# Two gates' clamp on GpSimd, a later start of layer 0's first attention head, and another order of the last sums, in a two-layer hybrid decoder

## The chip, the cores and the metric

The kernel runs on one core of a Trainium2 chip. The metric is the device time of one execution in microseconds (us), the median over the runs; smaller is better. Engines are named as in the profile: PE is the matrix engine (TensorE) and PEld its weight loads, DVE is VectorE, ACT is ScalarE, POOL is GpSimd, SP is SyncE, which issues most DMAs.

## What is computed

Two layers over 528 tokens (16 learned meta tokens and 512 real ones) with 1024 features, all in float32. The reference, cut to what matters:

```python
def hybrid_layer(h, attn_norm_g, w_in, b_fgate, ret_gn_g, w_out, ...):
    xn = rmsnorm(h, attn_norm_g)
    proj = jnp.einsum('bld,dc->blc', xn, w_in)
    fq, fk, fv, flog, rq, rk, rv, rg = jnp.split(proj, SPLIT_POINTS, axis=-1)
    logf = jax.nn.log_sigmoid(flog + b_fgate)
    fox_out = fox_attention(fq, fk, fv, logf)        # 8 heads of 64: softmax with a decay
    rq_ = rotate(rq, cos, sin)
    rk_ = rotate(rk, cos, sin) * (RET_HEAD_DIM ** -0.5)
    ret = retention_chunkwise(rq_, rk_, rv)          # 4 heads of 128: no softmax
    ret = head_groupnorm(ret, ret_gn_g)
    ret_out = jax.nn.silu(rg) * ret
    h = h + jnp.einsum('blc,cd->bld', jnp.concatenate([fox_out, ret_out], -1), w_out)
    hn = rmsnorm(h, ffn_norm_g)
    ff = jax.nn.silu(hn @ w_gate) * (hn @ w_up)
    return h + ff @ w_down

def reference(x, meta_tokens, ...):
    ...
    for i in range(DEPTH):
        h = hybrid_layer(h, ...)
    return rmsnorm(h, final_norm)[:, N_META:]
```

## The kernel before

Features lie on the 128 partitions and tokens along the free dimension. Each float32 operand is split into a high part, rounded to the fp32r type, and a low part, and a product takes three matmuls: high by high, high by low, low by high. A dense projection (L225) is a row of eight *chunks*, one per 128 input features. In layer 0 a chunk is six matmuls, three products for each of two halves of 264 tokens; in layer 1, where only the 512 real tokens go on, a chunk of some projections is three matmuls of 512 columns.

**Weights.** A DMA on SP brings a weight block to `raw`; ACT rounds it to `whi` in two halves (L199), and for most projections of the attention stage POOL subtracts `wlo = raw - whi` in eight pieces of 128 columns (L202). This is called ahead for the next projection, so that PE finds the parts ready.

**Attention.** A pair of softmax heads ("fox") is cut into steps: `scores` for the queries of one head and one block (PE L524 into a PSUM tile of the ring `psa`, which has four buffers; DVE L528 subtracts the mask and finds the row's minimum `nmax`; ACT L541 takes exponentials), `values` (PE transposes L427 of `pd`; ACT L505 and DVE L506 split them into `vv`), `turn` (PE transposes of the exponentials `pr`; ACT L150 and DVE L151 split them into `pth`, `ptl`), and `product` (PE L594, then ACT L597 and DVE L598). The keys `kc` of a head carry the forget gates' sums, put there by DVE L472 or ACT L469 for the first pair and by POOL L467 for the later ones.

**Retention.** A head's steps are `values` (transposes L427; DVE L690 takes means and L691 subtracts them), `scores` (PE L727; DVE L732 multiplies by the decay into `sd`; ACT L150 and DVE L151 split it into `rsh`, `rsl`), `product` (PE L761), then `weigh`, `head_norm` and `gate`. The gate projection of a head ends in `g_done` (L653): DVE L655 scales it into `sg`. For heads 2 and 3 ACT then applies silu. For heads 0 and 1, which run beside softmax exponentials, silu is built from exponentials: DVE L664 writes `ge = max(sg, -80)`, ACT L665 takes `exp(-ge)`, L666 a logarithm and L667 an exponential. The clamp keeps the exponential finite. Heads 0 and 1 run in each of the two layers, so L664 runs four times.

**Order.** PE runs exactly the order of the written plan. A list of dense chunks is the base, and `merge` puts the other steps in front of the chunk with the number that stands as their place; `spread(main, a, b)` spaces the first part of a fox pair's steps evenly from place a to b, and `ret_places` gives each step of a retention head its place. For the other engines a scheduler orders instructions by its own estimates, except those that are pinned; each engine then runs its own order strictly, waiting at an instruction for its semaphores.

**The end.** The last norm takes its statistics in two parts of 272 and 240 tokens. For the second, ACT squares each of the eight blocks `h[m]` (`square_b`, L1140). DVE adds some of the squares into an accumulator (`sum_b`, L1143); the accumulator and the remaining squares are added over partitions by plain float32 matmuls with a matrix of ones (L1169), each of which is two passes on PE. ACT takes the root (L1157), DVE refines it in three instructions (L1161, L1163, L1165) and multiplies the output (L1147), and SP stores it.

Of the kernel before, what the change touches and what calls it, by code (L numbers as in the profile page):

```python
# [13 lines left out]
ALU = mybir.AluOpType  # L14

D = 1024
NK = D // 128
# [22 lines left out]
def hybrid_kernel(ctx, tc, x_t, w_in, w_fl, w_out, w_gate, w_up, w_down, vecs, b_fg, rope, decay, mask, ident, out_t):  # L40
    nc = tc.nc
# [75 lines left out]
    def repeat(vt, c0, n, at):  # L117
        nc.scalar.copy(vt[:, at:at + 32 * n].rearrange("p (n c) -> p n c", c=32)[:, :, 0:META],
                       vt[:, c0:c0 + META].unsqueeze(1).broadcast_to([128, n, META]))
# [10 lines left out]
    def sv(t, real, p0=0, p1=128):  # L130
        if real:
            return t[p0:p1, META:T]
        return t[p0:p1, 0:T].rearrange("p (a b) -> p a b", a=2)

    def pv(ps, real, p0=0, p1=128):
        if real:
            return ps[p0:p1, 0, 0:SEQ]
        return ps[p0:p1, :, 0:HALF]
# [10 lines left out]
    def split(hi, lo, src, pinned=False):  # L149
        pin(nc.scalar.copy(hi, src), pinned)  # L150
        pin(nc.vector.tensor_sub(lo, src, hi.bitcast(F32)), pinned)  # L151
# [53 lines left out]
    def dense_steps(src, parts, pool=False, banks=False, ahead=(1, 4), own=None, wait=None):  # L205

        j = len(jobs)
        jobs.append({"src": src, "pool": pool, "own": own})  # L210

        def chunk(k0, k, n, xs, cols, ps, done):
            def go():
                convert(j)
                if k == 0:
                    t = [psum_a() for _ in cols] if banks else psum()
                    ps.append(t)
                    ps.append(t if banks else [t[:, b] for b in range(2)])
                size = jobs[j]["w"][0][0]
                _, hi, lo = jobs[j]["w"][(k0 + k) // size]  # L220
                wk = (k0 + k) % size
                xh, xl = xs(k)
                for i, (w, x) in enumerate(((hi, xh), (hi, xl), (lo, xh))):
                    for b, (c0, c1) in enumerate(cols):
                        nc.tensor.matmul(ps[1][b][:, 0:c1 - c0], w[:, wk, :], x[:, c0:c1],  # L225
                                         start=(k == 0 and i == 0), stop=(k == n - 1 and i == 2))
                if k == n - 1:
                    done(ps[0]) if wait is None else wait.append((ps[0], done))
                for half, at_step in enumerate(ahead):
                    if k0 + k == at_step:  # L230
                        convert(j + 1, 4 * half + 4)
            return go

        steps = []
        for k0, xs, n, cols, done in parts:
            ps = []
            steps += [chunk(k0, k, n, xs, cols, ps, done) for k in range(n)]
        return steps
# [35 lines left out]
    def tt(name, dt=F32):  # L274
        tag, bufs = tags[name]
        return tmp.tile([128, T], dt, name=name, tag=tag, bufs=bufs)

    def at(tag, dt=F32R, shape=(128, T), bufs=None):
        return phase["att"].tile(list(shape), dt, name=tag, tag=tag, bufs=bufs)

    def fft(tag, dt=F32R, shape=(128, T), bufs=None):
        return phase["ffn"].tile(list(shape), dt, name=tag, tag=tag, bufs=bufs)
# [32 lines left out]
    def pin(f, pinned=True):  # L315
        if pinned:
            tc.keep_in_program_order(f)
# [97 lines left out]
    def silu(t, then=None):  # L415
        nc.scalar.activation(t, t, AF.Silu)
        if then:
            tc.keep_in_program_order(nc.scalar.preload_act_table_set(then))
# [210 lines left out]
    def ret_dense(l, hd, ly, real, st, which):  # L629
        QC = REAL if real else FULL  # L630

        def rope_done(nm, rl):
            def go(ps):
                xsw = tt("xsw")
                nc.scalar.copy(sv(xsw, rl, 0, 64), pv(ps, rl, 64, 128))
                nc.scalar.copy(sv(xsw, rl, 64, 128), pv(ps, rl, 0, 64))
                nc.vector.tensor_mul(sv(xsw, rl), sv(xsw, rl), sv(ly["sr"], rl))
                t1 = tt("tq")
                nc.vector.tensor_mul(sv(t1, rl), pv(ps, rl), sv(ly["cr"], rl))
                nc.vector.tensor_add(sv(t1, rl), sv(t1, rl), sv(xsw, rl))  # L640
                th = at(nm + "h")
                tl = at(nm + "l")
                split(sv(th, rl), sv(tl, rl), sv(t1, rl))
                st[nm] = (th, tl)
            return go

        def v_done(ps):
            vr = v_tiles[1]
            nc.vector.scalar_tensor_tensor(sv(vr, False), pv(ps, False), RSC, sv(ly["R"], False), ALU.mult, ALU.mult)
            repeat(vr, SEQ, 2, SEQ + 32)  # L650
            st["vr"] = vr

        def g_done(ps):  # L653
            sg = tt("sg")
            nc.vector.scalar_tensor_tensor(sv(sg, real), pv(ps, real), RSC, sv(ly["R"], real), ALU.mult, ALU.mult)  # L655
            st["sg"] = sg
            if hd > 1:
                silu(sv(sg, real), LOGS)
                return


            u, v = sv(tt("ge"), real), sv(at("gr", F32), real)
            x = sv(sg, real)
            nc.vector.scalar_tensor_tensor(u, x, -80.0, x, ALU.max, ALU.max)  # L664
            nc.scalar.activation(u, u, AF.Exp, scale=-1.0)  # L665
            nc.scalar.activation(v, u, AF.Ln, bias=onec)  # L666
            nc.scalar.activation(v, v, AF.Exp, scale=-1.0)  # L667
            st["open"] = u, v, x

        base = 3 * FP + 4 * hd  # L670
        job = {"q": (0, QC, rope_done("rq", real)), "k": (1, FULL, rope_done("rk", False)),
               "v": (2, FULL, v_done), "g": (3, QC, g_done)}
        return sum([dense_steps(w_in[l, base + job[c][0]], [(0, lambda k: ly["x"][k], NK, job[c][1], job[c][2])], True)
                    for c in which], [])
# [150 lines left out]
    def ffn(l, st, real, last):  # L825
# [235 lines left out]
        for r, (f0, f1) in enumerate(ROUNDS):  # L1061
            for f in range(f0, f1):
# [4 lines left out]
                u = Unit(f)  # L1067
# [27 lines left out]
        else:  # L1095
# [4 lines left out]
            na, nb = PA[1] - PA[0], PB[1] - PB[0]  # L1100
            fin = {}
# [28 lines left out]
            def square_b(m):  # L1130
                if m == 0:
                    t = fft("S", F32, (128, 6, w), 2)
                    fin["one"] = [t[:, i, 0:nb] for i in range(2)]
                    fin["acc"], fin["rb"], fin["tb"] = (t[:, i, 0:nb] for i in range(3, 6))
                    d = fin["acc"]
                elif m < NK - 2:
                    fin["sq", m] = d = tt("sq")[:, 0:nb]
                else:
                    d = fin["one"][m - NK + 2]
                pin(nc.scalar.activation(d, h[m][:, cb], AF.Square))  # L1140

            def sum_b(m):
                pin(nc.vector.tensor_add(fin["acc"], fin["acc"], fin["sq", m]))  # L1143
# [23 lines left out]
            def sums(v, parts):  # L1167
                for i, t in enumerate(parts):
                    nc.tensor.matmul(v, ones if t.dtype == F32R else ones.bitcast(F32), t, start=(i == 0), stop=(i == len(parts) - 1))  # L1169
# [51 lines left out]

            def after_7():
                square_b(7)
                sum_b(5)
                v = psum_a()[:, 0:nb]
                sums(v, [fin["one"][0], fin["acc"], fin["one"][1]])
                out_a(2)
                out_a(4)
                out_a(6)
                scale_b(3)  # L1230
                root(fin["rb"], v)
                scale_b(4, 5, 6, 7)
                for i in range(3):
                    newton(i, fin["rb"], v, fin["tb"])
                for k in range(0, NK, 2):
                    out_b(k)

            end = NK * n
            places = [(end, after_a)] + [(end + n * (i + 1), f) for i, f in enumerate(
                (after_0, after_1, after_2, after_3, after_4, after_5, after_6, after_7))]  # L1240
# [11 lines left out]
    def layer(l):  # L1252
# [57 lines left out]
        q, k, v = fd(0)  # L1310
# [19 lines left out]
        sums = [lambda: forget_sums(l, ly)]  # L1330
# [11 lines left out]

        for g in range(2):
            main, rest = fs[g]
            m0, r0, places = (((7 if l else 11, 31 if l else 32.5), (34, 40.5), (13, 33.5, 35.5, 37.5, 39, 40.5, 43, 44, 47.5, 48)),
                              ((0.5, 31.5), (32, 40), (13, 33.5, 35.5, 39.5, 39, 41.5, 43, 44, 47.5, 48)))[g]
            plan += merge(rd(g, "vqkg") + sum(fd(g + 1), []),
                          spread(main, *m0), spread(rest, *r0), ret_places(g, *places))
# [92 lines left out]
```

## Time and profile before

| | |
|---|---|
| median of 3 runs | 1268.45 us (1268.43 to 1269.03) |
| the profiled execution's own time | 1268.51 us |
| its span, from the first to the last instruction | 1266.7 us |
| mean granted TensorE clock | 0.998 |
| busy: PE / PEld / DVE / ACT / POOL | 99% / 94% / 79% / 56% / 22% |
| read from HBM, written | 112.58 MB, 2.10 MB |

The span is what the trace covers; 1.8 us of the execution's time lie around it. In a row of the timeline the columns are the start and the duration in us, the engine, the line in the kernel, the operation, what is written and read, the shapes, how many instructions are merged into the row, and in brackets the engine's idle time in front of it and what ended it. A row of the waits names the engine that waited, the line at which it waited and for whom, then the sum, the number and the longest of the waits.

### The profile page before, as it was taken

The page shows a single profiled execution, that of the slowest core. Times are in us where ns is not written, and L with a number is a line of the kernel's source. Part 1 is how long each engine was busy: PE and PEld are TensorE (multiplying, and loading weights), DVE is VectorE, ACT ScalarE, POOL GpSimd, SP SyncE. Part 2 cuts the span into 40 slices and gives each one's busy share as a digit, 9 for nine tenths or more (in the row PEclk, how much of TensorE's full clock was granted, in tenths as well). Part 3 has the DMA queues.
Part 4 walks back from the last instruction along what each step waited for, and adds up shares of the span by engine and source line. Part 5 has one row for each costly group of instructions (what it writes and reads, how often), then busy time and mean ns, then how long its engine had stood idle before and what let it go on. Part 6 is the DMA issues. An engine that isn't in the chain of part 4 may idle for free.

```text
span 1266.7 us, 23528 instructions
## 1 busy us (share of the span) xinstructions
PE 1250.7 (99%) x9223; PEld 1192.2 (94%) x9223; DVE 994.4 (79%) x1800; ACT 706.2 (56%) x1305; POOL 274.3 (22%) x540
## 2 busy tenths in 40 slices
PE   9999999999999999999999999999999999999997
PEld 9999999999999999999999989998789999999996
DVE  8887756879988888887786877567899888888867
ACT  7767655676444444444466665557764444444445
POOL 3555546420000000000126556554100000000000
PEclk9999999999999999999999999999999999999999
DMA  6212222223333333332322122222233333333321
GB/s 218 67 60 69 83 76 73 71 67 117 105 97 100 100 101 100 101 101 84 101 77 84 61 84 74 71 89 67 100 96 121 100 101 101 100 101 101 100 84 67
DMA packets 43342, 116.19 MB, mean 92 GB/s; under 512 B 5088, under 2 KB 12000, under 8 KB 43232
## 3 DMA queue, kind: packets, MB, share of 16 engines
q1 hardware_dynamic: 42800, 114.41, 28.1%
q8 instruction: 72, 1.18, 0.4%
q14 instruction: 38, 0.31, 0.1%
q10 hardware_dynamic: 432, 0.29, 0.1%
HBM read 112.58 MB, written 2.10 MB: 91 GB/s over the span
## 4 chain that ended last, share of the span: by engine, by line
PE 91%; DVE 4%; ACT 4%; issue 1%; DMA 0%; ACTq 0%; DVEq 0%
PE psd L225 28%; PE psa L912 18%; PE psd L1047 14%; PE psd L912 13%; PE psa L225 5%; PE psa L1047 4%; PE psa L427 2%; PE psa L524 1%; PE psa L594 1%; PE psa L761 1%; PE psa L727 1%; ACT whi L199 1%; PE psa L298 0%; ACT xh L327 0%; DMA raw<-w_in 0%
## 5 line engine op out<-in xcount | busy, mean ns | idle before, releaser
L202 POOL TENSOR_TENSOR wlo<-raw,whi 128x128 fp32r<-128x128 f32 x504 | 259.1, 548 | 256.0 <-ACT whi L199 235.3
L225 PE MATMUL psd<-xh,whi 128*128 128x264 f32 (+1 forms) x792 | 195.5, 314 | 0.0
L225 PE MATMUL psd<-xh,wlo 128*128 128x264 f32 (+1 forms) x792 | 186.9, 304 | 0.0
L225 PE MATMUL psd<-xl,whi 128*128 128x264 f32 (+1 forms) x792 | 186.4, 303 | 0.4 <-DVE xl L328 0.4
L225 PEld LDWEIGHTS psd<-xh,whi 128*128 128x128 f32 x792 | 128.5, 190 | 4.9 <-ACT whi L199 0.5
L225 PEld LDWEIGHTS psd<-xh,wlo 128*128 128x128 f32 x792 | 127.0, 188 | 6.3 <-DVE wlo L202 0.4
L225 PEld LDWEIGHTS psd<-xl,whi 128*128 128x128 f32 x792 | 127.6, 189 | 5.1 <-DVE xl L328 1.1
L199 ACT CAST whi<-raw 128x512 fp32r<-128x512 f32 (+1 forms) x168 | 97.9, 613 | 41.7 <-PE psd L225 28.6
L900 ACT CAST whi<-raw 128x1024 fp32r<-128x1024 f32 (+2 forms) x62 | 54.8, 885 | 51.2 <-PE psd L912 39.8
L900 ACT CAST fwhi<-raw 128x1024 fp32r<-128x1024 f32 (+2 forms) x62 | 55.6, 897 | 48.0 <-PE psd L912 40.5
L122 POOL MEMSET kc<- 64x528 f32 x2 | 1.1, 532 | 345.4 <-PE psa L912 345.4
L901 DVE TENSOR_TENSOR wlo<-raw,whi 128x1024 fp32r<-128x1024 f32 (+2 forms) x62 | 62.9, 1015 | 12.6 <-ACT whi L900 12.5
L901 DVE TENSOR_TENSOR fwlo<-raw,fwhi 128x1024 fp32r<-128x1024 f32 (+2 forms) x62 | 64.0, 1033 | 11.0 <-ACT fwhi L900 10.7
L912 PE MATMUL psa<-th,whi 128*128 128x264 f32 (+1 forms) x232 | 65.4, 282 | 0.0
L912 PE MATMUL psa<-th,wlo 128*128 128x264 f32 (+1 forms) x232 | 65.4, 282 | 0.0
L912 PE MATMUL psa<-tl,whi 128*128 128x264 f32 (+1 forms) x232 | 65.3, 282 | 0.0
L912 PE MATMUL psa<-th,fwhi 128*128 128x264 f32 (+1 forms) x224 | 63.4, 283 | 0.0
L912 PE MATMUL psa<-tl,fwhi 128*128 128x264 f32 (+1 forms) x224 | 63.3, 283 | 0.0
L912 PE MATMUL psa<-th,fwlo 128*128 128x264 f32 (+1 forms) x224 | 63.2, 282 | 0.0
L541 ACT ACTIVATE pr<-pr,nmax 128x144 f32<-128x144 f32 (+1 forms) x64 | 36.8, 575 | 44.4 <-DVE nmax L528 25.7
L900 ACT CAST fwhi<-S 128x1024 fp32r<-128x1024 f32 x20 | 21.0, 1049 | 68.6 <-PE psa L912 66.5
L978 ACT COPY e<-psa 128x264 f32<-128x264 f32 (+1 forms) x114 | 42.9, 376 | 28.3 <-PE psa L912 24.1
(368 smaller groups left out, 4044.8 us busy)
## 6 DMA issues: line engine op xcount, KB each, us to landing
raw<-w_in SPq DMA_DIRECT2D x54, 512.0 KB, 3.5
raw<-w_gate SPq DMA_DIRECT2D x44, 512.0 KB, 4.0
fraw<-w_up SPq DMA_DIRECT2D x38, 512.0 KB, 3.5
raw<-w_down SPq DMA_DIRECT2D x64, 256.0 KB, 2.9
raw<-w_out SPq DMA_DIRECT2D x16, 512.0 KB, 3.5
raw<-w_down SPq DMA_DIRECT2D x32, 192.0 KB, 2.5
raw<-w_up SPq DMA_DIRECT2D x6, 512.0 KB, 3.5
h<-x_t SPq DMA_DIRECT2D x8, 264.0 KB, 4.5
```

The costliest lines, as they stand in the source:

```text
L199: pin(nc.scalar.copy(hi, job["raw"][:, c0:c1]), pinned)
L202: pin(sub(lo[:, c:c + step], job["raw"][:, c0 + c:c0 + c + step], hi[:, c:c + step].bitcast(F32)), pinned)
L225: nc.tensor.matmul(ps[1][b][:, 0:c1 - c0], w[:, wk, :], x[:, c0:c1], start=(k == 0 and i == 0), stop=(k == n - 1 and i == 2))
L427: nc.tensor.transpose(ps[:, 128 * j:128 * j + 128], src[:, o:o + 128], idt)
L524: nc.tensor.matmul(sc[0:nq, 0:c1 - c0], qq[:, q0:q0 + nq], kk[:, c0:c1], start=(i == 0), stop=(i == 1))
L541: nc.scalar.activation(pr, pr, AF.Exp, bias=nmax[0:nq], scale=-1.0, accum_out=rsum)
L594: nc.tensor.matmul(po[:, c0:SEQ], v[:, j, :], pp[:, j, META + c0:T], start=(j == 0 and i == 0), stop=(j == 4))
L900: nc.scalar.copy(hi, src)
L901: nc.vector.tensor_sub(lo, src, hi.bitcast(F32))
L912: nc.tensor.matmul(bank()[:, 0:b.shape[-1]], a[:, o + k, :], b, start=(fresh and k == 0 and i == 0), stop=(k == n - 1 and i == 2), skip_gr ...
L978: nc.scalar.copy(self.t["e"][:, i], self.t["x"][:, 0:w])
L1047: nc.tensor.matmul(v[:, 0:c1 - c0], a[:, s * n + k, :], b[:, c0:c1], start=(k == 0 and i == 0), stop=(k == n - 1 and i == 2))
```

## The change

Three edits. The clamp L664 moves from DVE to POOL, and from an instruction that reads `sg` twice to one that reads it once with a constant. In layer 0 the first fox pair's steps start at place 12 instead of 11 and end at 33 instead of 32.5, and the first retention head's `values` moves from place 13 to 16.5; layer 1 keeps its places. At the end three squares (of blocks 5, 6 and 7) instead of two (6 and 7) go to PE as they are, so DVE makes one addition less and PE one float32 matmul more.

```diff
-            nc.vector.scalar_tensor_tensor(u, x, -80.0, x, ALU.max, ALU.max)
+            nc.gpsimd.tensor_scalar_max(u, x, -80.0)
...
-                    fin["one"] = [t[:, i, 0:nb] for i in range(2)]
+                    fin["one"] = [t[:, i, 0:nb] for i in range(3)]
...
-                elif m < NK - 2:
+                elif m < NK - 3:
                     fin["sq", m] = d = tt("sq")[:, 0:nb]
                 else:
-                    d = fin["one"][m - NK + 2]
+                    d = fin["one"][m - NK + 3]
...
                 square_b(7)
-                sum_b(5)
                 v = psum_a()[:, 0:nb]
-                sums(v, [fin["one"][0], fin["acc"], fin["one"][1]])
+                sums(v, [fin["one"][0], fin["acc"]] + fin["one"][1:])
...
-            m0, r0, places = (((7 if l else 11, 31 if l else 32.5), (34, 40.5), (13, 33.5, 35.5, 37.5, 39, 40.5, 43, 44, 47.5, 48)),
+            m0, r0, places = (((7 if l else 12, 31 if l else 33), (34, 40.5), (13 if l else 16.5, 33.5, 35.5, 37.5, 39, 40.5, 43, 44, 47.5, 48)),
```

What this does to the engines' orders, at three places. First PE in layer 0, where the first fox pair begins. `psd` rows are dense chunks (two rows of high weights and one of low weights make one chunk), `kc` rows are the scores of the pair's first head, `pd_115` are the fox values and `pd_116` the retention values.

```order
-L524 MATMUL psa<-kc_105,qo_103 16x16
-L524 MATMUL psa<-kx_462,qs_453 16x16
 L225 MATMUL psd<-xh_185,whi 128x264 x2
 L225 MATMUL psd<-xl_186,whi 128x264 x2
 L225 MATMUL psd<-xh_185,wlo 128x264 x2
+L524 MATMUL psa<-kc_105,qo_103 16x16
+L524 MATMUL psa<-kx_462,qs_453 16x16
 L225 MATMUL psd<-xh_193,whi 128x264 x2
 L225 MATMUL psd<-xl_194,whi 128x264 x2
 L225 MATMUL psd<-xh_193,wlo 128x264 x2
```

The first scores stand one chunk later, and so do the pair's following steps up to its first `product`; the retention values, which stood right behind the 128x144 scores, now stand behind the 128x272 scores and one more chunk. From the scores that follow that product on, PE's order is the same as before up to the end.

Second, POOL in layer 1, at the gate of the first retention head: the eight pieces of one weight block are a run of eight rows of L202.

```order
 L467 TENSOR_SCALAR kc_8392<-fs,pick 40x528
-L202 TENSOR_TENSOR wlo<-raw,whi 128x128 x40
+L202 TENSOR_TENSOR wlo<-raw,whi 128x128 x8
+L664 TENSOR_SCALAR ge<-sg 128x512
+L202 TENSOR_TENSOR wlo<-raw,whi 128x128 x32
```

The clamp stands behind a whole weight block of eight pieces. In layer 0 the first clamp stands in the same way behind the eight pieces that follow `kc_106`; the second head's clamps stand behind one piece in layer 0 and two in layer 1.

Third, ACT at the same place in layer 1; these rows are the changed kernel's, and before, ACT had them in this order too, with the last two the other way round.

```order
L575 CAST pth<-pe 16x4x16
L665 ACTIVATE ge<-ge 128x512
L150 CAST pth<-psa 128x2x128
L666 ACTIVATE gr<-ge,onec 128x512
L150 CAST rsh<-sd 128x512
L667 ACTIVATE gr<-gr 128x512
L150 CAST pth<-psa 128x3x128
L150 CAST rsh<-sd 128x400
```

L665 now waits for POOL instead of DVE, and the cast to `rsh`, which PE's first retention product L761 needs, is queued behind it. At the same place in layer 0 ACT had L665, L541, L666, L551, L667, `rsh`; it now has L541, L665, L551, L666, `rsh`, L667.

## The prediction

> **What bounds the kernel now.** I read the page's first part and the chain of work that ended last, then the stages, then what PE waited for in each stage.
>
> ```profile
> PE 1250.7 (99%) x9223; PEld 1192.2 (94%) x9223; DVE 994.4 (79%) x1800; ACT 706.2 (56%) x1305; POOL 274.3 (22%) x540
> PE 91%; DVE 4%; ACT 4%; issue 1%; DMA 0%; ACTq 0%; DVEq 0%
> 275.35 20.64 PE psd L225 x168
> 30.00:80.00 50.00, 46.04 (x362) 43.95 (x361) 41.51 (x99) 34.82 (x86) 23.02 (x46) 1.00 0.18 59
> 690.00:710.00 20.00, 19.72 (x117) 17.11 (x116) 15.56 (x33) 13.62 (x30) 9.12 (x18) 1.00 0.21 67
> ```
>
> PE is busy 99% of the span and carries 91% of the chain. Its work is fixed by the plan and hardly changes here. So nothing counts but the gaps in PE's row, and the tail behind its last matmul. DVE's and POOL's busy time alone are worth nothing. The chain's third row gives PE's pace: 168 matmuls in 20.64 us, 0.123 us each, so a chunk of six is 0.73 us. The two stages show where the change can act: PE idles 50.00 - 46.04 = 3.96 us between 30 and 80 us (layer 0, first pair), and 0.28 us between 690 and 710 us (the same place in layer 1). These are PE's waits there, in the order stage of layer 0 (eight rows), layer 1 (one), end (one):
>
> ```profile
> PE psa L727 <- DVE ptl L151: 1.0, 1, 1.0
> PE psa L524 <- DVE kc L472: 0.8, 1, 0.8
> PE psa L594 <- DVE ptl L151: 0.7, 1, 0.7
> PE psa L427 <- DVE sd L732: 0.4, 1, 0.4
> PE psa L524 <- DVE sq L691: 0.4, 1, 0.4
> PE psa L761 <- DVE rsl L151: 0.2, 1, 0.2
> PE psa L761 <- ACT rsh L150: 0.2, 1, 0.2
> PE psa L427 <- DVE nmax L528: 0.2, 1, 0.2
> PE psa L761 <- DVE rsl L151: 0.3, 1, 0.3
> PE psa L1169 <- ACT S L1140: 0.9, 1, 0.9
> ```
>
> A stall costs about 0.2 to 0.25 us more than its idle time. A matmul stands in the record with some 0.3 us, although the next one starts 0.12 us behind it.
>
> **Layer 0 up to the product.** The pair's first scores waited for `kc` (0.8 idle, about 0.95 lost). Now a further chunk, 0.73, stands in front of them, while `kc` comes when it did: 0.2 stays, gain 0.75. The next two waits (0.2 for `nmax`, 0.4 for the retention values' L691, together about 1.05 lost) were for PSUM buffers that the retention values had taken between the fox scores. They now come behind two more steps, but new short waits replace them: the fifth retention transpose needs the 128x272 scores reduced, and the 128x400 scores need the fox values' last split. I walked DVE and ACT in their new order with the durations of their rows and get 0.15 and 0.35: gain 0.55. The product's wait for the last `ptl` (0.7 idle, 0.95 lost) has one more chunk in front of it, and its inputs follow from the same scores some 1.3 us earlier, behind a DVE row relieved of the retention values' early place; I take all of it, with 0.5 us to spare. Together 0.75 + 0.55 + 0.95 = **2.25 us** by the time PE reaches the second head's last scores; bounds 0.75 (the two unsure parts give nothing) and 2.7.
>
> **Layer 0, the clamp.** From those scores on PE's order is unchanged:
>
> ```profile
> 61.02 0.28 PE L524 MATMUL psa<-kc,qo 128*128 128x264 f32 x1
> 61.65 0.70 POOL L467 TENSOR_SCALAR kc<-fs,pick 40x528 fp32r<-40x528 f32 x1 [4.20 <-PE psa L524]
> 62.32 3.38 POOL L202 TENSOR_TENSOR wlo<-raw,whi 128x128 fp32r<-128x128 f32 x8
> 62.55 3.72 DVE L664 SCALAR_TENSOR_TENSOR ge<-sg 128x528 f32<-128x528 f32 x1
> 66.30 0.64 ACT L665 ACTIVATE ge<-ge 128x528 f32<-128x528 f32 x1 [3.50 <-DVE ge L664]
> 67.57 0.72 ACT L666 ACTIVATE gr<-ge,onec 128x528 f32<-128x528 f32 x1
> 68.31 0.62 ACT L551 COPY tq<-sums 128x512 f32<-128x512 f32 x1
> 69.38 0.62 ACT L150 CAST rsh<-sd 128x528 fp32r<-128x528 f32 x1
> 70.79 0.50 PE L761 MATMUL psa<-rsl,rvh 128*128 128x512 f32 x1 [0.25 <-DVE rsl L151]
> L664 DVE SCALAR_TENSOR_TENSOR ge<-sg x4: 658/795/3722, 62.5 to 750.2; 128x528 f32<-128x528 f32 x2, 128x512 f32<-128x512 f32 x2
> L467 POOL TENSOR_SCALAR kc<-fs,pick x12: 697/703/1157, 47.2 to 798.5; 40x528 fp32r<-40x528 f32 x12
> L373 POOL MEMSET mxh<- 128x512 f32 x2 | 1.1, 525 | 6.0 <-PE psd L1047 6.0
> ```
>
> One of the four clamps took 3.72 us, the others 0.66 to 0.92. It lay beside POOL's eight weight pieces (62.32 to 65.70) and ended after them. Behind it DVE could not finish `ptl`, which let PE wait 1.0 us at L727, and ACT stood 3.50 us. On POOL the clamp is not in the trace. The nearest row is L467, also one SBUF input and constants, 528 elements per partition: 0.70 us, which I take. The ends are 0.53 (the memset, which reads nothing) and 1.16 (L467's longest).
>
> [...]
>
> Now the clamp waits on POOL for the eight pieces. From the scores: 0.63 to `kc`, 0.67 for it, 3.34 for the pieces, 0.70 for the clamp, 0.05 to ACT, then L665, L551 and L666 (starts 0.55 to 0.7 apart, 1.87), `rsh` 0.62, and 0.79 to the second L761 (`rsl` on DVE and the two handovers): 8.67 us. Before it was 70.79 - 61.02 = 9.77. **Gain 1.1 us**, 0.6 to 1.3 with the clamp's ends. The waits at L727 and L427 vanish, but most of what they gave comes back as a wait for `rsh`: PE reaches L761 at about 65.4 and `rsh` is there at 66.7.
>
> **Layer 1, the clamp.** There the old clamp was short, and nothing hides the new queue:
>
> ```profile
> 697.37 0.67 DVE L655 SCALAR_TENSOR_TENSOR sg<-psd,R 128x512 f32<-128x512 f32 x1
> 697.43 3.97 POOL L202 TENSOR_TENSOR wlo<-raw,whi 128x128 fp32r<-128x128 f32 x8 [4.33 <-ACT whi L199]
> 698.29 0.67 DVE L664 SCALAR_TENSOR_TENSOR ge<-sg 128x512 f32<-128x512 f32 x1
> 699.00 0.63 ACT L665 ACTIVATE ge<-ge 128x512 f32<-128x512 f32 x1 [1.00 <-DVE ge L664]
> 700.41 0.61 ACT L150 CAST rsh<-sd 128x512 fp32r<-128x512 f32 x1
> 701.32 0.40 PE L761 MATMUL psa<-rsh,rvh 128*128 128x512 f32 x1
> 702.00 0.50 PE L761 MATMUL psa<-rsl,rvh 128*128 128x512 f32 x1 [0.28 <-DVE rsl L151]
> ```
>
> `sg` is ready at 698.04, but POOL first runs its eight pieces, to 697.43 + 3.38 = 700.81 once DVE's clamp no longer stretches one of them. The clamp ends at 701.51 and L665 starts at 701.55, not 699.00. Queued behind L665 on ACT are the `pth` cast, L666 and `rsh`, so `rsh` ends at 700.41 + 0.61 + 2.55 = 703.57. PE is at L761 by 701.32 and waits until 703.62. `rsl` takes 0.7 more, so the second L761 starts at 704.35 instead of 702.00: **loss 2.35 us**, 2.2 to 2.8 with the clamp's ends, 2.9 if the pieces keep their 3.97.
>
> **The second head's clamps** cost nothing:
>
> ```profile
> 120.79 4.42 POOL L202 TENSOR_TENSOR wlo<-raw,whi 128x128 fp32r<-128x128 f32 x8 [1.57 <-ACT whi L199]
> 122.20 0.66 ACT L665 ACTIVATE ge<-ge 128x528 f32<-128x528 f32 x1
> 749.71 3.84 POOL L202 TENSOR_TENSOR wlo<-raw,whi 128x128 fp32r<-128x128 f32 x8 [1.42 <-ACT whi L199]
> 751.52 0.63 ACT L665 ACTIVATE ge<-ge 128x512 f32<-128x512 f32 x1
> ```
>
> Behind one piece (0.43) the clamp ends near 121.9, behind two near 751.3. Both are before ACT reaches L665 behind other work. The later pieces end no more than 0.4 us later than before, and PE waits for no `wlo` anywhere.
>
> **The end.** PE's last sums are moved forward by what they no longer wait for:
>
> ```profile
> 1256.28 0.39 ACT L1140 ACTIVATE sq<-h 128x240 f32<-128x240 f32 x1
> 1257.39 1.48 PE L1169 MATMUL psa<-S,ones 128*128 128x240 f32 x6 [0.89 <-ACT S L1140]
> ```
>
> The six passes start 0.2 us apart, after square 6. With square 5 first they start at 1256.71 and are eight: the last starts about 1256.71 + 0.31 + 6 x 0.2 = 1258.23 against 1258.51 now. Square 7 (ready at 1257.63) is needed at 1257.92. **Gain 0.3 us**, bounds 0 and 0.4; root and output follow unchanged.
>
> **Sum.** -2.25 - 1.1 + 2.35 - 0.3 = -1.3 us on the profiled execution's 1268.51 (span 1266.7, 1.8 around it, unchanged), 1267.2. That execution lies 0.06 above the median of 1268.45, so the forecast is **1267.2**.
>
> **Rivals.**
> - *Layer 1 does not pay.* If `rsh` is not held, because the pieces run early enough that POOL is free when `sg` comes, the loss goes: -3.65, so 1264.8. Against it: the pieces' start is set by ACT's casts, at 697.43, within 0.1 us of `sg`'s own start. This is the only way to over 0.2%; 0.2% of the time is 2.5 us, about what a measurement can tell from no change. Chance 0.18.
> - *New waits replace the old ones at layer 0's start.* The buffers of `psa` are still four; if the fox values and the retention transposes collide as before and the product still waits, only 0.75 of the 2.25 stays: +0.2, so 1268.7. Chance 0.15, within 0.2%.
> - *The clamp is slow on POOL* (slower than before). Each further us of it costs 2 us, since PE waits behind it once in each layer; from 0.70 + 0.65 = 1.35 us on the kernel is slower. If the time went with partitions, 128 instead of L467's 40, it would be 2.24 us, the sum +1.8, 1270.3; with little gained at layer 0's start as well, 1271.8. For it: no POOL row with 128 partitions and one input exists. Against: the memsets take 0.53 with 64 partitions and with 128. Chance 0.17: 0.05 for the first time, within 0.2%, and 0.12 for the second, over it.
> - *The clamp meets DVE.* L467 at 747 us took 1.16 instead of 0.70 beside DVE. So each deciding clamp could be 0.46 longer: +0.9, 1268.1. Chance 0.1. [...]
>
> **How the numbers follow.** The forecast itself has 0.40. Within 0.2% are it, the second and fourth rival and the third's first time: 0.40 + 0.15 + 0.10 + 0.05 = 0.70. Faster 0.18, slower 0.12. The range of 8 in 10 takes in the first rival's time and the third's first one, and leaves out the third's second (0.12) and what lies below the first rival (some 0.06): 1264.6 to 1270.3.
>
> **What would show it.** Right: PE's wait for `kc` under 0.1 idle; no wait at L594 and L727; L761 in layer 0 waiting about 1.1 idle for `rsh`; L761 in layer 1 about 2.1; L664 on POOL near 0.70; eight passes of L1169 from half a us earlier. Wrong: a clamp over 1.3 us, a wait at L594 that stays, or no wait at L761 in layer 1.

## The result, and the profile after

| | before | after |
|---|---|---|
| median, 12 runs each | 1268.82 us (1268.43 to 1269.83) | 1271.51 us (1269.29 to 1272.28) |
| profiled execution, its span | 1268.51, 1266.7 | 1271.55, 1269.8 |

The ratio is 1.002, with a 95% interval of 1.0013 to 1.0028: slower, by 2.7 us. Forecast were 1267.2 us and a range up to 1270.3.

PE runs the same matmuls in the same order outside the moved places, so one row in two traces tells where time went. The shift of such rows against before, from PE's rows in the timelines:

| row | before | after | shift | so this part gave | forecast |
|---|---|---|---|---|---|
| last `psa<-xh,mxl` pair, ahead of every edit | 28.44 | 28.81 | +0.37 | (start of this one execution) | 0 |
| second head's last scores (L524) | 61.02 | 59.87 | -1.15 | places: -1.52 | -2.25 |
| second L761, layer 0 | 70.79 | 69.31 | -1.48 | clamp, layer 0: -0.33 | -1.1 |
| second L761, layer 1 | 702.00 | 703.70 | +1.70 | clamp, layer 1, the wait: +3.1 | +2.35 |
| `xl` wait at L225 | 914.95 | 918.32 | +3.37 | behind that wait: +1.6 | 0 |
| end of L1169 | 1258.87 | 1261.94 | +3.07 | end order: -0.30 | -0.3 |

Without the start, the last column but one adds up to 2.6 us. With a drift of 0.1 between 70 and 700 us, which the fourth part leaves out, that is the 2.7 between the medians. The end order did what was forecast. Three parts did not.

**Layer 1.** The stage's rows in the timeline of after, DVE's `sg`, then POOL, ACT and PE (start, duration, and in brackets the idle time before the row with what ended it):

```profile
695.98 0.67 DVE L655 SCALAR_TENSOR_TENSOR sg<-psd,R 128x512 f32<-128x512 f32 x1
696.03 3.38 POOL L202 TENSOR_TENSOR wlo<-raw,whi 128x128 fp32r<-128x128 f32 x8 [4.33 <-ACT whi L199]
699.38 1.49 POOL L664 TENSOR_SCALAR ge<-sg 128x512 f32<-128x512 f32 x1
700.91 0.63 ACT L665 ACTIVATE ge<-ge 128x512 f32<-128x512 f32 x1 [4.30 <-POOL ge L664]
702.32 0.60 ACT L150 CAST rsh<-sd 128x512 fp32r<-128x512 f32 x1
702.98 0.50 PE L761 MATMUL psa<-rsh,rvh 128*128 128x512 f32 x1 [2.86 <-ACT rsh L150]
703.70 0.50 PE L761 MATMUL psa<-rsl,rvh 128*128 128x512 f32 x1 [0.23 <-DVE rsl L151]
704.33 0.63 PE L225 MATMUL psd<-xh,whi 128*128 128x512 f32 x1
704.75 0.63 PE L225 MATMUL psd<-xl,whi 128*128 128x512 f32 x1
```

The chain is the forecast one: `sg` at 696.65, eight pieces to 699.41, the clamp, L665, `rsh`, L761. Only the clamp takes 1.49 us where 0.70 was assumed, and PE's wait is 2.86 instead of 2.3. The last two rows show something else. A chunk's matmul of 128x512 starts 0.23 us behind the one before it in the trace of before; here rows of 0.63 us follow, 0.42 to 0.43 apart. The spacing in before:

```profile
698.36 0.39 PE L225 MATMUL psd<-xh,whi 128*128 128x512 f32 x1
698.59 0.39 PE L225 MATMUL psd<-xl,whi 128*128 128x512 f32 x1
```

The windows of after say why; their columns are span, busy time of PE, PEld, DVE, ACT and POOL with counts, then the granted TensorE clock, DMA share and GB/s:

```profile
703.00:704.00 1.00, 0.77 (x2) 0.46 (x3) 1.00 (x2) 0.82 (x2) 0.00 (x0) 1.00 0.00 0
704.00:705.00 1.00, 1.00 (x4) 0.76 (x3) 0.87 (x3) 0.53 (x1) 0.00 (x0) 0.60 0.00 0
705.00:706.00 1.00, 1.00 (x4) 0.71 (x4) 0.30 (x1) 0.00 (x0) 0.00 (x0) 0.50 0.00 0
706.00:707.00 1.00, 1.00 (x7) 1.00 (x6) 0.00 (x0) 0.30 (x1) 0.00 (x0) 0.50 0.00 0
707.00:708.00 1.00, 1.00 (x9) 1.00 (x9) 0.68 (x2) 0.29 (x1) 0.00 (x0) 0.70 0.00 0
```

The clock is at half for 0.8 + 1 + 1 + 0.6 = 3.4 us, and work done at half speed for 3.4 us is 1.7 us late. PE shows as fully busy there: from 705 to 706 us its share is 1.00 with four matmuls at a clock of 0.50, and e3 below has 1.00 with twelve at 1.00.

**Layer 0.** What PE waited for between 30 and 80 us in after, and the rows behind it:

```profile
PE psa L727 <- DVE ptl L151: 0.9, 1, 0.9
PE psa L761 <- ACT rsh L150: 0.3, 1, 0.3
PE psa L427 <- ACT vv L505: 0.3, 1, 0.3
PE psa L761 <- DVE rsl L151: 0.3, 1, 0.3
```

```profile
59.87 0.28 PE L524 MATMUL psa<-kc,qo 128*128 128x264 f32 x1
61.18 3.38 POOL L202 TENSOR_TENSOR wlo<-raw,whi 128x128 fp32r<-128x128 f32 x8
62.04 3.13 DVE L533 TENSOR_TENSOR nmax<-nmax 128x1 f32<-128x1 f32 x1
64.53 1.52 POOL L664 TENSOR_SCALAR ge<-sg 128x528 f32<-128x528 f32 x1
65.26 0.74 ACT L541 ACTIVATE pr<-pr,nmax 128x528 f32<-128x528 f32 x1 [3.60 <-DVE nmax L533]
65.42 0.46 PE L727 MATMUL psa<-rqh,rkh 128*128 128x400 f32 x1 [0.92 <-DVE ptl L151]
66.09 0.65 ACT L665 ACTIVATE ge<-ge 128x528 f32<-128x528 f32 x1
69.31 0.50 PE L761 MATMUL psa<-rsl,rvh 128*128 128x512 f32 x1 [0.25 <-DVE rsl L151]
```

The waits for `kc`, and at L594, are gone from the list, as forecast. The one at L727 is not. With the clamp off DVE, the hold of three microseconds fell on the next DVE instruction with two SBUF inputs: L533, the smaller of two columns of 128x1, took 3.13 us (L655, which reads `psd` in PSUM, took 0.69 beside the same pieces). Behind it stand `ptl` and the exponential L541, so PE waits for `ptl` and ACT for `nmax`, as before. But this hold isn't what sets the second L761 here: L665 needs the clamp, which ends on POOL at 66.05, and it starts at 66.09.

At the end PE's wait for the squares is 0.21 instead of 0.89, with eight passes:

```profile
1260.05 1.89 PE L1169 MATMUL psa<-S,ones 128*128 128x240 f32 x8 [0.21 <-ACT S L1140]
```

### The profile page after: what moved, and what is told of

It is laid out like the page before. It is cut to its first block, busy times and chain, and to the rows that moved or that the text cites. A ratio compares the mean times of both kernels' runs of the same rounds, so it can differ in the third digit from the quotient of the medians.

```text
span 1269.8 us, 23537 instructions
## 1 busy us (share of the span) xinstructions
PE 1252.6 (99%) x9225; PEld 1193.5 (94%) x9225; DVE 990.5 (78%) x1795; ACT 706.6 (56%) x1305; POOL 279.2 (22%) x544
## 5 line engine op out<-in xcount | busy, mean ns | idle before, releaser
L202 POOL TENSOR_TENSOR wlo<-raw,whi 128x128 fp32r<-128x128 f32 x504 | 258.3, 548 | 255.4 <-ACT whi L199 226.0
L225 PE MATMUL psd<-xh,whi 128*128 128x264 f32 (+1 forms) x792 | 195.4, 314 | 0.8 <-ACT whi L199 0.8
L225 PE MATMUL psd<-xh,wlo 128*128 128x264 f32 (+1 forms) x792 | 186.9, 303 | 0.0
L225 PE MATMUL psd<-xl,whi 128*128 128x264 f32 (+1 forms) x792 | 186.4, 302 | 0.4 <-DVE xl L328 0.4
L225 PEld LDWEIGHTS psd<-xh,whi 128*128 128x128 f32 x792 | 128.1, 189 | 5.6 <-ACT whi L199 1.3
L225 PEld LDWEIGHTS psd<-xh,wlo 128*128 128x128 f32 x792 | 126.9, 188 | 6.4 <-DVE wlo L202 0.6
L225 PEld LDWEIGHTS psd<-xl,whi 128*128 128x128 f32 x792 | 127.5, 189 | 4.9 <-DVE xl L328 0.8
L541 ACT ACTIVATE pr<-pr,nmax 128x144 f32<-128x144 f32 (+1 forms) x64 | 36.8, 576 | 49.0 <-DVE nmax L528 27.0
```

The costliest lines, as they stand in the source:

```text
L202: pin(sub(lo[:, c:c + step], job["raw"][:, c0 + c:c0 + c + step], hi[:, c:c + step].bitcast(F32)), pinned)
L541: nc.scalar.activation(pr, pr, AF.Exp, bias=nmax[0:nq], scale=-1.0, accum_out=rsum)
```

## The experiments

Theory A: the loss is layer 1's alone, made of the eight pieces ahead of the clamp on POOL, of POOL's price of 1.5 us, and of the lowered clock behind a long wait; in layer 0 POOL's pieces hold whichever two-input instruction of DVE comes up, so taking the clamp off DVE gained little. The rivals stand in the expectations. The table below has each kernel's time, and by the shift of PE's rows against before, in the profiled execution, what each part gave:

| kernel | median us (runs) | places | clamp, layer 0 | layer 1 | end | start |
|---|---|---|---|---|---|---|
| after | 1271.51 (12) | -1.52 | -0.34 | +4.67 | -0.29 | +0.38 |
| e1 all clamps on DVE | 1266.13 (11) | -1.50 | -0.94 | +0.01 | -0.26 | -0.05 |
| e2 before, clamps on POOL | 1271.05 (11) | +0.05 | -2.41 | +4.54 | 0.00 | +0.88 |
| e3 wait filled | 1270.00 (11) | -1.46 | -0.34 | +3.07 | -0.26 | +0.20 |
| e5 L533 with one input | 1265.91 (11) | -1.50 | -1.10 | +0.08 | -0.29 | +0.44 |
| e6 and clamp with one input | 1265.41 (9) | -1.52 | -1.38 | -0.19 | -0.27 | -0.21 |
| e7 first clamps ahead of the pieces | 1265.14 (6) | -1.55 | -2.76 | +0.77 | -0.29 | +0.07 |
| e8 one clamp on POOL, ahead | 1264.24 (5) | -1.48 | -2.78 | +0.04 | -0.27 | +0.74 |
| e11 e8, the others with one input | 1264.00 (5) | -1.46 | -2.78 | -0.27 | -0.27 | -0.23 |

The parts are read at rows near 80, 690 and 720 us and at the last ones, so they can differ by some 0.01 from the table above, and "layer 1" has the wait and what came behind it. "Clamp, layer 0" is everything between the second head's last scores and the rows at 80 us, so in e1 it is an effect of the new places. The column "start" is the shift ahead of every edit. It runs from -0.23 to +0.88 between single executions, so parts are read from one trace and whole kernels from medians.

**e1: the clamps back on DVE**

```diff
-            nc.gpsimd.tensor_scalar_max(u, x, -80.0)
+            nc.vector.scalar_tensor_tensor(u, x, -80.0, x, ALU.max, ALU.max)
```

> The changed kernel with all four clamps back on DVE in their old form; the new places of layer 0 and the new end stay. Theory A (layer 1's first clamp on POOL is the whole loss: POOL's price of 1.5 us, the eight pieces ahead of it, and a lower granted TensorE clock behind the wait): layer 1 comes back whole, 4.67 us by the two traces, and layer 0 keeps what the trace of after shows, 1.87, the end 0.28: 1268.8 - 1.9 - 0.3 = 1266.6 us. In layer 0 the combination of the score minima (L533) is still held some 3.1 us on DVE by POOL's pieces, since it comes ahead of the clamp there. Rival B (the old clamp was what POOL's pieces held, so layer 0 falls back with it): the clamp takes over 3 us again at 62 us and at least 0.35 of the gain goes, 1267.0 or more. Rival C (the moved places cost time later): 1268 or more.

1266.13 us (ratio to before 0.9978, 0.9969 to 0.9987). Layer 1 came back whole: its loss is the clamp's on POOL, and rival C falls. In layer 0 L533 is held and the clamp behind it is not, in the timeline of e1:

```profile
60.77 3.38 POOL L202 TENSOR_TENSOR wlo<-raw,whi 128x128 fp32r<-128x128 f32 x8
61.63 2.54 DVE L533 TENSOR_TENSOR nmax<-nmax 128x1 f32<-128x1 f32 x1
64.30 0.69 DVE L664 SCALAR_TENSOR_TENSOR ge<-sg 128x528 f32<-128x528 f32 x1
```

Rival B falls too: the hold stays with the instruction that comes first. L533 ends at 64.17, with the last piece (64.15). In after it ended 0.61 behind the last piece, while the clamp ran on POOL. So in layer 0 as well the move of the clamp to POOL, behind the pieces, cost time: -0.34 with it, -0.94 without.

**e2: before with the clamps on POOL**

The diff of e1 turned round, on the kernel before.

> The kernel before with nothing but the four clamps on POOL. Theory A: layer 1 loses what it lost in after, 4.67 (3.0 of waiting and 1.6 of lower clock); layer 0 gains little, 0.3 at most, since another two-input DVE instruction is held in the clamp's place: 1268.8 + 4.4 = 1273.2 us. Rival B (layer 0 had its gain from the clamp's leaving DVE): layer 0 gains 1.1 or more, 1272.4 or less. Rival D (no clock effect, the rows behind the wait are slow for another reason that the new places bring): 1271.6.

1271.05 us (ratio 1.0016, 1.0007 to 1.0024). Layer 1 lost 4.54, as expected, but layer 0 gained 2.41, not 0.3. My figure was wrong, and rival B's, which fell in e1, was nearest in size. The timeline of e2 gives the reason:

```profile
63.26 1.52 POOL L664 TENSOR_SCALAR ge<-sg 128x528 f32<-128x528 f32 x1
63.59 0.30 DVE L533 TENSOR_TENSOR nmax<-nmax 128x1 f32<-128x1 f32 x1
64.76 3.39 POOL L202 TENSOR_TENSOR wlo<-raw,whi 128x128 fp32r<-128x128 f32 x8
```

With the old places the scheduler put the clamp ahead of the pieces in POOL's queue. The pieces came 1.5 us later, and L533 was through before them. In after the same edit stands behind the pieces. In layer 0 each part of the change by itself gains 2.4 (the clamp in e2: 2.41 less 0.05; the places in e1: 1.50 and 0.94). Both together gave 1.86, so the clamp's move is a gain of 2.4 with the old places and a loss of 0.6 with the new ones.

**e3: the wait in layer 1 filled**

```diff
             po, d = st["po"], st["d"]
+            if l and hd == 0 and grp[0] == 0:
+                for _ in range(12):
+                    nc.tensor.matmul(po, vh[:, 0, :], st["rq"][0][:, META:T], start=True, stop=True)
```

> The changed kernel with twelve more matmuls of 128x512 in layer 1's first head, put on PE just ahead of the retention product that waits for the clamp. They work on operands that are ready and write a bank that the product then starts anew, so they add nothing to the result; they only keep PE at work while it would wait. Theory A (the long idle stretch lowers the clock for the 3.4 us behind it): the granted clock stays at 1.00 and the product's rows take 0.23 us instead of 0.43; the wait itself stays in time. 1271.5 - 1.6 = 1269.9 us. Rival D (the rows behind the wait are slow for another reason, such as the late weights or ACT's and DVE's queues): the rows stay slow, 1271.5 us or a little more.

1270.00 us, 1.5 below after. The product waits as long in time, but the granted clock stays, in the windows of e3:

```profile
704.00:705.00 1.00, 1.00 (x7) 0.76 (x6) 0.87 (x3) 0.53 (x1) 0.00 (x0) 1.00 0.00 0
705.00:706.00 1.00, 1.00 (x12) 1.00 (x11) 0.21 (x1) 0.48 (x1) 0.00 (x0) 1.00 0.00 0
706.00:707.00 1.00, 1.00 (x10) 0.87 (x10) 0.86 (x2) 0.29 (x2) 0.00 (x0) 1.00 0.00 0
```

Layer 1's loss falls from 4.67 to 3.07. So 1.6 us were the clock's, and idle time, not late operands, brought them: rival D falls.

**e4: the price of POOL's forms**

24 instructions on a copy of one tile, where POOL is idle (lines of e4's own numbering):

```diff
+                        nc.gpsimd.tensor_scalar_max(o, s0, -80.0)
+                        nc.gpsimd.tensor_scalar_max(o[0:40], s0[0:40], -80.0)
...
+                        nc.gpsimd.tensor_scalar(o, s0, ones[:, 0:1], 0.0, ALU.mult, ALU.add)
+                        nc.gpsimd.tensor_scalar(o[0:40], s0[0:40], ones[0:40, 0:1], 0.0, ALU.mult, ALU.add)
+                        nc.gpsimd.tensor_scalar(o, s0, -80.0, 0.0, ALU.max, ALU.add)
...
```

> The changed kernel with 24 more GpSimd instructions in layer 0's feed-forward part, where POOL has nothing else to do: eight forms three times each, from a copy of one tile into a tile that nothing reads. Forms: L856 max with a constant 128x512, L857 the same with 40 partitions, L858 the same 128x128, L859 multiply by a column and add 128x512, L860 the same with 40 partitions (the form of L467), L861 max and add 128x512, L862 product of two inputs 128x512, L863 difference of two inputs 128x128 (the form of the weight pieces). The time is not of interest. Theory A1 (the operation sets the price: a max is slow on POOL): L856, L857 and L861 near 1.5 us, L859 and L860 near 0.7. Rival A2 (the partitions set it): L856, L859 and L861 near 1.5, L857 and L860 near 0.7. Rival A3 (the clamp was slow because DVE worked beside it): the shortest L856 is near 0.7.

Shortest, median and longest of three, in ns, by line in e4:

```profile
L856 POOL TENSOR_SCALAR probe<-psrc x3: 1806/1883/3058, 317.4 to 344.5; 128x512 f32<-128x512 f32 x3
L857 POOL TENSOR_SCALAR probe<-psrc x3: 1478/1479/1480, 320.6 to 346.3; 40x512 f32<-40x512 f32 x3
L859 POOL TENSOR_SCALAR probe<-psrc,ones x3: 699/1479/2083, 322.8 to 348.6; 128x512 f32<-128x512 f32 x3
L860 POOL TENSOR_SCALAR probe<-psrc,ones x3: 1014/1515/2049, 324.9 to 349.4; 40x512 f32<-40x512 f32 x3
L861 POOL TENSOR_SCALAR probe<-psrc x3: 2255/2705/2896, 326.5 to 351.5; 128x512 f32<-128x512 f32 x3
```

DVE was busy beside most of them, and the times of one row spread (L859 from 0.70 to 2.08 us), so the shortest count. A maximum takes 1.48 us with 40 partitions and 1.49 (after's L664) with 128. A multiplication with an addition, on 128 partitions, takes 0.70. So the partitions don't set the price. Theory A1's operation does, or another difference of the two forms that no run separates from it: the multiplication takes its factor from a column, the maximum a constant. Not all is as theory A1 had it: the maximum with an addition is dearer still, 2.26 at the shortest, no L860 came undisturbed (1.01 at the shortest, against L467's 0.70 in before), and the shortest L856 is 1.81, over after's 1.49.

**e5 and e6: fewer inputs on DVE**

e5 is e1 with the first edit, e6 has the second as well:

```diff
-                nc.vector.tensor_tensor(nmax, mins[0], mins[1], ALU.min)
+                nc.vector.tensor_scalar(nmax, mins[0], mins[1], None, ALU.min)
...
-            nc.vector.scalar_tensor_tensor(u, x, -80.0, x, ALU.max, ALU.max)
+            nc.vector.tensor_scalar_max(u, x, -80.0)
```

> The kernel of e1 (all clamps on DVE, 1266.13 us) with one more edit: the minimum of the two score minima (L533, 128x1) takes its second input as a per-partition scalar, so that it is an instruction with one tensor input. Behind it DVE now comes at once to the old clamp, which names the tile of sg twice. Theory H (any DVE instruction with two SBUF inputs that comes up while POOL works through its eight pieces is held until the last of them is done): L533 takes under 0.2 us, the hold goes over to the clamp, which takes about 3 us and ends about 0.6 us behind the last piece, and PE waits at L727 for ptl as before: 1265.9 us, hardly better. Rival S (the 3 us of L533 were not POOL's, but a wait for its own inputs): L533 stays at 2.5 us or more, 1266.1.

1265.91 us. L533 is free, and the clamp behind it is held in its place, in e5:

```profile
62.12 0.20 DVE L533 TENSOR_SCALAR nmax<-nmax 128x1 f32<-128x1 f32 x1
62.24 2.97 DVE L664 SCALAR_TENSOR_TENSOR ge<-sg 128x528 f32<-128x528 f32 x1
```

Theory H is right to the number, and rival S falls.

> The kernel of e5, and the four clamps on DVE as a maximum with a constant, one input instead of two. Theory H: nothing in layer 0's first head is held any more; L533 under 0.2 us, the clamp 0.7 us or less, while the eight pieces run; the waits at L727 and L427 go, and some of those at L761: 1.0 to 1.6 us better than e1, 1264.5 to 1265.1. Rival P (a one-input instruction of DVE from SBUF to SBUF is held too): the clamp takes about 3 us again, 1265.9. [...]

1265.41 us, between the two forecasts. By the rows the rival wins: the clamp with one input is held too, in e6 (the last row is the same clamp in layer 1, not held):

```profile
61.45 0.20 DVE L533 TENSOR_SCALAR nmax<-nmax 128x1 f32<-128x1 f32 x1
61.57 2.69 DVE L664 TENSOR_SCALAR ge<-sg 128x528 f32<-128x528 f32 x1
695.32 0.41 DVE L664 TENSOR_SCALAR ge<-sg 128x512 f32<-128x512 f32 x1
```

Theory H is too narrow: the clamp took 2.69 us with one tensor input and 2.97 with two (e5), so it isn't the count of tensor inputs alone. The part of the gain that came is, against e5, 0.3 in layer 0 and 0.3 in layer 1.

**e7 and e8: the clamp ahead of the pieces**

e7 pins the first head's clamp and the pieces of the weights behind it in program order on POOL, in both layers. e8 does so in layer 0 only and has the other clamps on DVE in the old form.

```diff
-            nc.gpsimd.tensor_scalar_max(u, x, -80.0)
+            pin(nc.gpsimd.tensor_scalar_max(u, x, -80.0), hd == 0)
...
-                pin(sub(lo[:, c:c + step], job["raw"][:, c0 + c:c0 + c + step], hi[:, c:c + step].bitcast(F32)), pinned)
+                pin(sub(lo[:, c:c + step], job["raw"][:, c0 + c:c0 + c + step], hi[:, c:c + step].bitcast(F32)), pinned or job.get('first'))
```

> The changed kernel with the first head's clamp put ahead of the eight weight pieces in POOL's queue, in both layers; the other two clamps stay on POOL where they are. Theory A (in layer 1 the queue, 2.7 us of it, and the lower clock that comes from the long wait are most of the loss; POOL's price of 1.5 us alone is little): layer 1 loses 0.6 instead of 4.67, the granted clock stays at 1.00; layer 0 keeps the 1.5 of the places and gains up to the 2.4 that the clamp gave in e2, where it also stood ahead of the pieces, 3.5 together; the end 0.3: 1268.9 - 3.5 + 0.6 - 0.3 = 1265.7 us. Rival W (the pieces, now later, make PE wait for wlo): 1267 or more, with a wait for wlo in PE's row. Rival Q (the price, not the queue): layer 1 still loses 2 or more, 1267 or more.

1265.14 us (ratio 0.9971, 0.9960 to 0.9983). PE's waits in e7, first between 30 and 80 us, then between 690 and 710:

```profile
PE psa L427 <- ACT vv L505: 0.3, 1, 0.3
```

```profile
PE psa L761 <- DVE rsl L151: 0.5, 1, 0.5
PE psa L761 <- ACT rsh L150: 0.2, 1, 0.2
```

All that the list of layer 0 had from L727 on is gone, and PE waits nowhere for `wlo`. Layer 1 loses 0.77 instead of 4.67: that is what POOL's price alone costs; 3.9 were the queue and what it brought. Rivals W and Q fall. Layer 0 gained 4.3 in all (1.55 and 2.76) instead of 3.5, so the time is below the 1265.7 expected.

> The changed kernel with a single clamp on POOL, that of layer 0's first head, ahead of the eight pieces as in e7; the other three are back on DVE in the old form. Theory A: layer 0 as in e7 (3.5 gained), layer 1 as before the change, the end 0.3: 1268.9 - 3.8 = 1265.1 us, the best of these if e6's rival holds. Rival W: PE waits for wlo at 65 to 75 us, 1266 or more.

1264.24 us (ratio 0.9966, 0.9954 to 0.9979): layer 0 as in e7, layer 1 as before. For the same 4.3 it is below its 1265.1.

**e9 and e10: how long a wait lowers the clock**

e3 with `range(4)` and with `range(2)`.

> The kernel of e3 with four matmuls of 128x512 in the wait instead of twelve; each takes 0.23 us, so that 2.86 - 0.93 = about 1.9 us of idle time are left. Like those they add nothing to the result. Theory L (how long PE is idle decides whether the clock falls; 0.9 us in layer 0 did not do it, 2.86 did): no forecast for where between the two the point lies, but the runs are of one kind, with the clock at 1.00 and 1270.0 us, or with 0.5 behind the wait and 1271.5. Theory F (the chip looks at stretches of fixed length that run free of the kernel, so a wait of middle length lowers the clock in some executions and not in others; after had 11 runs near 1271.5 and one at 1269.3, the kernel of e2 nine near 1271.2 and two at 1269.4): a mixture, with more runs without the loss than after had; 1270.0 the median.

> The same with two matmuls: about 2.4 us idle are left. Theory L: as e9 or as after, whichever side of the point it lies on. Theory F: a mixture too, with more runs near 1271.5 than e9 has; the median 1271 us.

e9's profile shows a wait of 1.96 us with the clock at 1.00 behind it, e10's one of 2.41 with a lowered clock. The first row of each fence is the end of the wait, the second a microsecond behind it:

```profile
702.65 0.49 PE L764 MATMUL psa<-rsh,rvh 128*128 128x512 f32 x1 [1.96 <-ACT rsh L150]
704.00:705.00 1.00, 1.00 (x8) 0.81 (x7) 0.85 (x2) 0.37 (x1) 0.00 (x0) 1.00 0.00 0
```

```profile
703.11 0.80 PE L764 MATMUL psa<-rsh,rvh 128*128 128x512 f32 x1 [2.41 <-ACT rsh L150]
704.00:705.00 1.00, 1.00 (x3) 0.81 (x4) 0.87 (x3) 0.53 (x1) 0.00 (x0) 0.50 0.00 0
```

But one profile is one draw. The medians are 1270.51 us (e9, where 1270.0 was expected) and 1271.01 (e10). In these two kernels, after and e2, the times of all executions fall into two groups, with nothing between 1270.0 and 1270.8 us:

| kernel | idle at L761 | executions at 1269.3 to 1270.0 | at 1270.8 to 1272.3 |
|---|---|---|---|
| e9 | 1.96 | 5 | 5 |
| e10 | 2.41 | 4 | 6 |
| after | 2.86 | 1 | 11 |
| e2 | 2.89 | 2 | 9 |

Theory L falls: e9 and e10 are mixtures. Theory F is borne out, and 1.96 us of wait already cost in half of the executions. That the share grows with the wait goes by ten to twelve executions each; e9 and e10 differ by a single one. Each execution's mean granted clock was measured as well. It parts the groups in e9 (0.998 to 0.999, and 0.996 to 0.997 in the upper one), in e10 (0.999, and 0.996 to 0.998) and in after (0.999, and 0.995 to 0.998). In e2 it doesn't (0.997, and 0.995 to 0.997).

**e11: the best of both**

e8 with the three clamps on DVE as `tensor_scalar_max`.

> The kernel of e8 (1264.24 us) with the three clamps on DVE as a maximum with a constant, one input. In e6 the same form gained 0.2 in layer 1 (the shift there from -3.02 to -3.21 us), since it is shorter than the two-input form where nothing holds it: 1264.0 us. Rival P (it is held by POOL's pieces where the two-input form was not): 1264.3 or more.

1264.00 us (ratio 0.9962, 0.9948 to 0.9975), 7.5 us below after and 4.8 below before by the medians. Against e8 the runs overlap (1263.63 to 1264.37, and 1263.99 to 1265.30), so the step from e8 is shown only by layer 1's rows: -0.27 instead of +0.04.

## Why the prediction was wrong, point by point

- **The step that failed first** is the price in "The nearest row is L467, also one SBUF input and constants, 528 elements per partition: 0.70 us, which I take." The clamp took 1.49 to 1.54 us. I chose the row by shape and inputs; e4 shows that the partitions don't decide. L467 multiplies, by a column, where the clamp takes a maximum with a constant. On DVE the clamp took 0.66 in the old form (the shortest in before), and the same form as on POOL took 0.41 there (layer 1 of e6). The third rival had the mechanism (POOL slow, decided from 1.35 us) but sought it in the partitions. With 1.5 us for 0.70 my sum gives 0.8 more in each layer, 1268.8.
- **Layer 1, "loss 2.35 us".** The place, the queue of eight pieces and the waiting rows were as forecast. The wait came out at 3.1 by the price. The term that was missing is the clock: I reckoned a wait as costing its own length and some 0.2, and this one cost 1.6 more (e3). It was put at nothing because no row of the trace of before has a long wait of PE in the middle of its work. With that the sum is 1270.4.
- **Layer 0 up to the product, 2.25.** The gain is 1.5. By the shifts of PE's rows less the start, `kc` gave 0.72 of 0.75. The stretch from there to the product gave 0.15 of 0.55, with a new idle wait of 0.26 at L427 for the fox values, and the product 0.65 of 0.95. The bounds (0.75 to 2.7) held the sum. With 0.7 less the sum is 1271.1, and the measured median 1271.51.
- **"The waits at L727 and L427 vanish".** The one at L427 for `sd` did, the one at L727 stood at 0.92. I had asked what held the clamp, not whom POOL would hold next. The answer stands in e1, e5 and e6: L533, then the clamp again. This didn't move the sum: L727's 0.92 and L761's 0.29 are together the 1.1 or so that was forecast at L761. From the scores to the second L761 after took 9.44, where the forecast 8.67 with the price put right gives 9.5. More was there to be had in layer 0 (2.8 in e7), but only from a place ahead of the pieces, and with the new places the scheduler put the clamp behind them.
- **The second head's clamps: nothing.** Right: e7 keeps them on POOL, e8 does not, and their shifts between 80 and 690 us are the same; from 720 to 910 us they are within 0.02.
- **The end, 0.3.** Right: 0.29 in after, 0.26 to 0.29 in the others.
- **The chances.** "Slower by over 0.2%" had 0.12, and came, just (0.21%). It came by another way than the third rival's, which took POOL's time to go with partitions. The range left out two things that no row of the trace of before had priced: a maximum on POOL, and a long wait's second cost.

## What to carry to other kernels

Price an instruction on another engine by a row of the same operation and operands there, not of the same shape alone, and ask of each queue what stands ahead of the newcomer. Here, in layer 0 and with the new places, the clamp's move gained 1.8 us ahead of eight small instructions (e7 against e1) and lost 0.6 behind them (after against e1). When an instruction that a neighbour holds is taken away, find the next of its kind on the engine: here the hold passed on, from L664 (3.72 us in before) to L533 (3.13 in after) and back to L664 (2.97 in e5). And a wait on PE can be dearer than its length: waits of 1.96 to 2.89 us here were, in half (5 of 10 in e9) to nearly all (11 of 12 in after) of the executions, and in after this second cost was 1.6 us (e3).

## What the runs showed of the hardware

- **The clock.** Behind a wait of 2.86 us the granted clock stayed at 1.00 for another 1.2 us (PE was back at 702.98; the fall lies near 704.2) and was then at 0.50 for 3.4 us; in e10 it was low from the wait's end on, for 3.4 us too. In e9, whose profile has a wait of 1.96 us, the loss came in five of ten executions. The clock records in the traces, apart from their ends, suggest why. The low stretch of after lasts 3.413 us, and all their stretches are whole numbers of periods of that length: 367 in before (1252.69 us), then 205, the single low one, and 163 in after (699.73, 3.413 and 556.37 us). PE was idle for 2.42 us (after), 2.89 (e2), 2.62 (e4) and 2.27 (e10) of the period just ahead of it. Of the periods that left the clock at 1.00, the idlest in the thirteen traces has 1.38 (e9, whose wait lay across the end of a period at 702.08). So, as an estimate from these traces, the clock falls at a period's end when PE idled for somewhere between 1.4 and 2.3 us of it, and where in a period a wait lies would be luck. These are after's period ahead of the fall and its low one, then e9's:

```profile
700.78:704.20 3.42, 1.00 (x3) 0.64 (x4) 1.67 (x4) 2.95 (x7) 0.09 (x1) 1.00 0.40 139
704.20:707.61 3.41, 3.41 (x15) 2.93 (x14) 1.26 (x3) 1.08 (x2) 0.00 (x0) 0.50 0.00 0
698.66:702.08 3.42, 2.04 (x11) 1.39 (x9) 0.42 (x1) 1.50 (x4) 1.89 (x3) 1.00 0.41 153
```

- **The hold.** Beside POOL's run of eight pieces, at 61 to 65 us, one DVE instruction took 3.72 us (L664 in before), 3.13 (L533 in after), 2.54 (L533 in e1), 2.97 (L664 in e5) and 2.69 (L664 with one input, in e6), each until the run's end or up to 0.61 behind it. The minimum by a per-partition scalar on 128x1 (0.20) was not held. In layer 1 the same clamp form ran beside the same eight pieces in 0.67 us. What lets POOL pass all its pieces first at the one place and not at the other is not settled; no run tried it.
- **POOL's prices.** Maximum with a constant 1.48 to 1.54 us on 512 or 528 elements, with 40 or 128 partitions; multiply by a column and add 0.70; maximum and add 2.26 at the shortest, beside DVE's work. On DVE the maximum with a constant took 0.41 in layer 1 of e6.
